# Rows of cumulated decays: spread by matmuls, or fetched from DRAM over GpSimd's queue

## The chip, the cores and the metric

The kernel runs on one core of a Trainium2 chip. The metric is the device time of one execution in microseconds; of several runs the median is given.

## The reference

One residual layer of a streaming encoder on 1024 positions of width 1024, with 16 meta tokens ahead of them (1040 columns in all). Two token mixers work on the same normalised input: a Mamba-2 SSD (32 heads of 64 channels, 4 groups, state 128) and a gated DeltaNet (16 value heads, 8 query and key heads, 128 channels each). Their gated outputs are merged, projected and followed by a SwiGLU feed-forward block and a last RMSNorm. What matters here is one term of both mixers. Each head has a log decay per position, which is cumulated along a chunk, and inside a chunk every pair of positions l and s is weighted with the exponential of the difference:

```
diff = a_cum[..., :, None] - a_cum[..., None, :]
segsum_exp = jnp.exp(jnp.where(mask, diff, -jnp.inf))
scores = cb[:, :, :, None] * segsum_exp(a_cum)      # SSD
a_low = where(strict, (k_beta k^T) * decay, 0)      # DeltaNet, with decay = segsum_exp(g_cum)
qk = (q k^T) * decay
```

The kernel takes chunks of 128 positions: chunks 0 to 7, and chunk 8, which holds the 16 meta tokens and comes first.

## The kernel before, in words

**Stages.** The input is normalised and kept as two tiles, u_hi and u_lo, so that a product in float32 is made of three passes (`dense`, lines 143 to 145: high by high, low by high, high by low). First comes the tile with the decays and betas ("dab"), whose columns are turned into tokens by head (lines 308 to 356): the result is `cum` [128, 9, 48], the cumulated log decays of the 32 SSD heads and the 16 DeltaNet heads for nine chunks. Then DeltaNet runs in 8 sub-blocks of two value heads (`dn_conv`, `dn_p1`, `dn_inv`, `dn_meta`, `dn_merge`, `dn_p2`, `dn_z`), then SSD in 4 groups of 8 heads (`ssd_conv`, `ssd_chunk`, `ssd_z`, `ssd_norm`), then the branch projections, the output projection and the feed-forward block.

**Where the decay is made.** `decay` (line 420) needs, in every partition s, the row of cum over the positions l. The preparation (lines 359 to 374) transposes cum into rows, splits each row into three bf16 parts and stacks the parts in `rowS` and `rowD` [96, 1040]. In `decay` one matmul per head (line 424) multiplies a column of ones at that head's three rows, `selS` or `selD`, broadcast over 128 columns, with the chunk's part of the rows: every partition of a PSUM bank then holds the row. ScalarE computes the positive part of cum[s] - row[l] from PSUM into the tile E (line 427, Relu with scale -1 and bias cum) and then exp(-E) in place (line 430). In DeltaNet (`dn_p1`) the bank is shared with k k^T and k q^T, there are two heads per chunk, and E (eight buffers) lives until `dn_p2` of the same chunk has used it. In SSD (`ssd_chunk`) a chunk has two tiles Es of four heads each (three buffers), each from a bank of the tag "p"; ScalarE also makes `ec`, the exponential of the rows themselves, from the same bank (line 764), VectorE multiplies Es with the masked C B^T (line 765), and TensorE reads Es at line 777.

**What sets the order.** The program text gives priorities. The framework that builds the kernel places the instructions of each engine by these priorities, by data and buffers, and by its own forecast of durations; the order per engine is then fixed, each engine runs its queue in order, and semaphores are put in for dependences. So TensorE's queue is a mixture of a small step of DeltaNet or SSD and of dense products of other tiles that fill the gaps. Weight tiles come on SP's queue (`load_w`, line 135), with one tile ahead. GpSimd does little: in this part the memsets of raw (line 383), ss (445), X (556) and T32 (576).

**Chain of a DeltaNet sub-block.** `dn_p1` makes the blocks W of nine chunks, W goes to DRAM in 32 x 32 blocks (line 547), comes back as X (557), is inverted by 30 steps on VectorE (563, 565), goes out and back once more (567, 573), is merged on TensorE (593 to 612), and `dn_p2` runs through the chunks in order.

## Time and profile before

| | |
|---|---|
| median of 3 runs | 2938.79 us (2936.38 to 2939.13) |
| the profiled execution's own time | 2935.63 us |
| its span, first to last instruction | 2933.8 us |
| mean granted TensorE clock | 0.99 of full speed |
| TensorE / VectorE / ScalarE / GpSimd busy | 97% / 66% / 41% / 180 us |
| DMA | 227 MB, mean 77 GB/s |

In the views PE is TensorE's matmuls, PEld its weight loads (beside the matmuls), DVE VectorE, ACT ScalarE, POOL GpSimd, SP SyncE and SPq its queue of DMA issues. L424 is line 424 of the kernel. `out<-in` are tiles by the program's names, with partitions x elements and the type. A busy share is an average over stages, so stretches are read by themselves: start and end of a stretch in us from the span's start.

### The profile page before, as it was taken

The page shows a single profiled execution, that of the slowest core. Times are in us where ns is not written, and L with a number is a line of the kernel's source. Part 1 is how long each engine was busy: PE and PEld are TensorE (multiplying, and loading weights), DVE is VectorE, ACT ScalarE, POOL GpSimd, SP SyncE. Part 2 cuts the span into 40 slices and gives each one's busy share as a digit, 9 for nine tenths or more (in the row PEclk, how much of TensorE's full clock was granted, in tenths as well). Part 3 has the DMA queues.
Part 4 walks back from the last instruction along what each step waited for, and adds up shares of the span by engine and source line. Part 5 has one row for each costly group of instructions (what it writes and reads, how often), then busy time and mean ns, then how long its engine had stood idle before and what let it go on. Part 6 is the DMA issues. An engine that isn't in the chain of part 4 may idle for free.

```text
span 2933.8 us, 41854 instructions
## 1 busy us (share of the span) xinstructions
PE 2848.0 (97%) x15921; PEld 2420.8 (83%) x15921; DVE 1938.7 (66%) x3788; ACT 1203.0 (41%) x2856; POOL 180.4 (6%) x190
## 2 busy tenths in 40 slices
PE   8999999999999799999999999999999899999998
PEld 7888888898888689878888778888877788887887
DVE  7768687696876755867777653564668655556446
ACT  5645445354354344645555543222235233333212
POOL 2000000000000000000000000000100432230000
PEclk9999999999999999999999999999999999999999
DMA  3111121111211111121111124342453222226312
GB/s 101 51 58 44 44 66 37 51 52 30 73 44 44 60 50 44 37 71 38 51 45 47 69 80 158 108 160 91 138 167 105 98 81 86 86 79 223 97 50 83
DMA packets 120273, 227.27 MB, mean 77 GB/s; under 512 B 48088, under 2 KB 54904, under 8 KB 120072
## 3 DMA queue, kind: packets, MB, share of 16 engines
q1 hardware_dynamic: 119496, 224.07, 23.2%
q8 instruction: 125, 2.05, 0.3%
q14 instruction: 76, 0.62, 0.1%
q10 hardware_dynamic: 576, 0.52, 0.1%
HBM read 175.16 MB, written 49.38 MB: 77 GB/s over the span
## 4 chain that ended last, share of the span: by engine, by line
PE 83%; ACT 7%; DVE 6%; DMA 3%; issue 1%; SPq 0%; POOL 0%; DVEq 0%; POOLq 0%; ACTq 0%
PE psd L143 15%; PE psd L144 15%; PE psd L145 15%; PE pq_p L1038 1%; PE pq_p L1039 1%; PE pq_p L1040 1%; ACT Es L427 1%; PE ps_p L593 1%; PE pq_psd L1040 1%; PE pq_psd L1039 1%; PE pq_psd L1038 1%; PE ps_a L639 1%; PE ps_a L651 1%; PE ps_o L661 1%; PE ps_o L777 1%
## 5 line engine op out<-in xcount | busy, mean ns | idle before, releaser
L143 PE MATMUL psd<-u_hi,whi 128*128 128x512 f32 (+3 forms) x2136 | 759.8, 356 | 10.7 <-ACT raw L382 10.2
L144 PE MATMUL psd<-u_lo,whi 128*128 128x512 f32 (+3 forms) x2136 | 755.1, 354 | 3.7 <-DVE u_lo L152 2.7
L145 PE MATMUL psd<-u_hi,wlo 128*128 128x512 f32 (+3 forms) x2136 | 753.2, 353 | 1.7 <-DVE wlo L137 1.7
L143 PEld LDWEIGHTS psd<-u_hi,whi 128*128 128x128 f32 x2136 | 402.7, 189 | 51.7 <-ACT raw L382 15.9
L136 ACT CAST whi<-wraw 128x1024 fp32r<-128x1024 f32 (+2 forms) x197 | 187.9, 954 | 610.7 <-PE psd L144 430.0
L144 PEld LDWEIGHTS psd<-u_lo,whi 128*128 128x128 f32 x2136 | 402.8, 189 | 40.4 <-DVE u_lo L152 4.1
L145 PEld LDWEIGHTS psd<-u_hi,wlo 128*128 128x128 f32 x2136 | 403.2, 189 | 36.5 <-DVE wlo L137 2.4
L137 DVE TENSOR_TENSOR wlo<-wraw,whi 128x1024 fp32r<-128x1024 f32 (+2 forms) x197 | 219.0, 1112 | 121.0 <-ACT whi L136 118.6
L145 PE MATMUL psd<-blk,wlo 128*128 128x512 f32 x512 | 199.3, 389 | 0.0
L143 PE MATMUL psd<-blk,whi 128*128 128x512 f32 x512 | 199.2, 389 | 0.0
L144 PE MATMUL psd<-blk,whi 128*128 128x512 f32 x512 | 199.2, 389 | 0.0
L382 ACT COPY raw<-psd 128x256 f32<-128x256 f32 x165 | 73.2, 444 | 113.8 <-PE psd L145 111.8
L942 DVE TENSOR_TENSOR part<-part,psd 128x512 f32<-128x512 f32 x96 | 65.6, 683 | 74.3 <-PE psd L145 74.3
L145 PEld LDWEIGHTS psd<-blk,wlo 128*128 128x128 f32 x512 | 96.1, 188 | 20.2 <-DVE wlo L137 0.3
L144 PEld LDWEIGHTS psd<-blk,whi 128*128 128x128 f32 x512 | 96.1, 188 | 20.1
L143 PEld LDWEIGHTS psd<-blk,whi 128*128 128x128 f32 x512 | 96.1, 188 | 19.8
L1022 POOL TENSOR_TENSOR sw<-wraw 128x512 f32<-128x512 f32 x42 | 63.3, 1507 | 377.3 <-DMA wraw<-w_gu 377.3
L563 DVE TENSOR_TENSOR itmp<-X 66x30 f32<-66x30 f32 (+14 forms) x240 | 78.1, 326 | 6.5 <-DMA X<-nd 1.0
L565 DVE TENSOR_TENSOR X<-X,itmp 66x30 f32<-66x30 f32 (+14 forms) x240 | 78.1, 325 | 6.0
L427 ACT ACTIVATE Es<-ps_p,cum 128x128 f32<-128x128 f32 x256 | 73.5, 369 | 2.5 <-PE ps_p L424 1.7
L399 ACT ACTIVATE zt<-psd 128x512 f32<-128x512 f32 x64 | 38.1, 596 | 88.4 <-PE psd L145 66.1
L725 DVE TENSOR_TENSOR cbm<-ps_p,tri 128x128 f32<-128x128 f32 x32 | 9.3, 291 | 87.2 <-PE ps_p L723 87.0
(682 smaller groups left out, 5857.2 us busy)
## 6 DMA issues: line engine op xcount, KB each, us to landing
wraw<-w_in SPq DMA_DIRECT2D x105, 512.0 KB
wraw<-w_gu SPq DMA_DIRECT2D x48, 512.0 KB
wraw<-w_br SPq DMA_DIRECT2D x36, 512.0 KB
c<-hc SPq DMA_DIRECT2D x22, 512.0 KB
hc<-c SPq DMA_DIRECT2D x22, 512.0 KB
wraw<-w_dn SPq DMA_DIRECT2D x40, 256.0 KB
g<-zt SPq DMA_DIRECT2D x32, 256.0 KB
y_d<-zt SPq DMA_DIRECT2D x32, 256.0 KB
```

Source lines behind the costliest of these rows:

```text
L136: act.copy(hi[:, 0:kk], raw[:, 0:kk])
L137: dve.tensor_tensor(lo[:, 0:kk], raw[:, 0:kk], hi[:, 0:kk], op=ALU.subtract)
L143: pe.matmul(ps[:, 0:n], hi[:, wk0 + k], ahi(k), start=(k == 0), stop=False)
L144: pe.matmul(ps[:, 0:n], hi[:, wk0 + k], alo(k), start=False, stop=False)
L145: pe.matmul(ps[:, 0:n], lo[:, wk0 + k], ahi(k), start=False, stop=(k == kk - 1))
L382: dense_u((name, lambda ps, p0, p1: act.copy(raw[:, 3 + p0:3 + p1], ps)))
L427: act.activation(E[0:L, i, 0:L], ps[0:L, 128 * i:128 * i + L], AF.Relu, bias=cum[0:L, c, h0 + h:h0 + h + 1], scale=-1.0)
L563: dve.tensor_tensor(t, X[:, 0:j, j:j + 1].broadcast_to([66, j, m]), X[:, j:j + 1, j + 1:32].broadcast_to([66, j, m]), op=ALU.mult)
L565: dve.tensor_tensor(X[:, 0:j, j + 1:32], X[:, 0:j, j + 1:32], t, op=ALU.add)
L942: dve.tensor_tensor(part[:, m, cs], part[:, m, cs], ps, op=ALU.add)
L1022: eng.tensor_tensor(t, x, y, op=op)
L1038: pe.matmul(ps, w[0][:, k], y[0][:, k], start=start and k == 0, stop=False, skip_group_check=not start)
```

## The change

The preparation now makes only nine transposes of cum (48 heads at once), copies them into one tile of float32 rows, and stores it to a DRAM tensor of 48 rows. `spread` fetches the rows of n heads for one chunk with a DMA on GpSimd's queue straight into the tile E, broadcast over the partitions; `decay` then works in place on E. In DeltaNet `dn_rows` allocates E and issues the fetch; `dn_p1s` issues the first three chunks ahead of the first `dn_p1` and then the chunk two ahead. In SSD `ssd_rows` does the same for the next chunk ahead of the present one, with four buffers of Es in place of three, and `ec` is taken from the fetched rows before `decay` overwrites them. rowS, rowD, the selectors and their input are gone.

```
@@ body
+    cum_dram = dram.tile([48, TT], F32, name="cum_d")
...
-        for row, h0 in ((rowD, 16), (rowS, 0)):
-            c3 = sb.tile([128, 9, 3, 32], F32, name="c3")
-            pool.tensor_copy(c3, cum[:, :, h0:h0 + 32].unsqueeze(2).broadcast_to([128, 9, 3, 32]))
-            rr = sb.tile([96, TT], F32, name="rr")
-            b2 = sb.tile([96, TT], BF16, name="b2")
-            for c in range(9):
-                c0, L = (NM + 128 * c, 128) if c < 8 else (0, NM)
-                ps = psm("p")
-                pe.transpose(ps[0:96, 0:L], V(c3[0:L, c], "p a b -> p (a b)"), ident[0:L, 0:L])
-                act.copy(rr[:, c0:c0 + L], ps[0:96, 0:L])
-            for i in range(3):
-                r32 = slice(32 * i, 32 * i + 32)
-                act.copy(row[r32], rr[r32])
-                if i < 2:
-                    dve.tensor_copy(b2, rr)
-                    dve.tensor_tensor(rr, rr, b2, op=ALU.subtract)
+        rr = sb.tile([48, TT], F32, name="rr")
+        for c in range(9):
+            c0, L = (NM + 128 * c, 128) if c < 8 else (0, NM)
+            ps = psm("p")
+            pe.transpose(ps[0:48, 0:L], cum[0:L, c], ident[0:L, 0:L])
+            act.copy(rr[:, c0:c0 + L], ps[0:48, 0:L])
+        sp.dma_start(cum_dram, rr)
...
-    def decay(E, ps, row, sel, h0, hs, c):
+    def spread(E, h0, n, c):
         c0, L = cr(c)
-        for i, h in enumerate(hs):
-            pe.matmul(ps[0:L, 128 * i:128 * i + L], sel[:, h:h + 1].broadcast_to([96, L]),
-                      row[:, c0:c0 + L], start=True, stop=True)
-        for i, h in enumerate(hs):
-            act.activation(E[0:L, i, 0:L], ps[0:L, 128 * i:128 * i + L], AF.Relu,
-                           bias=cum[0:L, c, h0 + h:h0 + h + 1], scale=-1.0)
-        n = len(hs)
+        pool.dma_start(E[0:L, 0:n, 0:L], cum_dram[h0:h0 + n, c0:c0 + L].unsqueeze(0).broadcast_to([L, n, L]))
+
+    def decay(E, h0, n, c):
+        c0, L = cr(c)
+        for i in range(n):
+            act.activation(E[0:L, i, 0:L], E[0:L, i, 0:L], AF.Relu, bias=cum[0:L, c, h0 + i:h0 + i + 1], scale=-1.0)
         act.activation(E[0:L, 0:n, 0:L], E[0:L, 0:n, 0:L], AF.Exp, scale=-1.0)
...
+    def dn_rows(i, c):
+        E = sub[i]["E", c] = (sb.tile([128, 2, 128], F32, name="E", bufs=8) if c < 8 else
+                              sb.tile([NM, 2, NM], F32, name="Em"))
+        spread(E, 32 + 2 * i, 2, c)
@@ dn_p1
-            E = d["E", c] = sb.tile([128, 2, 128], F32, name="E", bufs=8)
-        else:
-            E = sb.tile([NM, 2, NM], F32, name="Em")
-        decay(E, ps, rowD, selD, 32, (2 * i, 2 * i + 1), c)
+        E = d["E", c]
+        decay(E, 32 + 2 * i, 2, c)
...
+    def ssd_rows(g, c):
+        if c == 8 or g == NGRP or (g, c) in ssd_E:
+            return
+        E = ssd_E[g, c] = [sb2.tile([128, 4, 128], F32, name="Es", bufs=4) for _ in range(2)]
+        for q in range(2):
+            spread(E[q], 8 * g + 4 * q, 4, c)
@@ ssd_chunk
+        ssd_rows(g, c)
+        ssd_rows(*((g, (c + 1) % 9) if c != 7 else (g + 1, 0)))
...
-        E = [sb2.tile([128, 4, 128], F32, name="Es", bufs=3) for _ in range(2)]
+        E = ssd_E.pop((g, c))
         for q in range(2):
-            pd = psm("p")
-            decay(E[q], pd, rowS, selS, 0, range(8 * g + 4 * q, 8 * g + 4 * q + 4), c)
-            pd = V(pd, "p (a b l) -> p a b l", a=2, b=2)
+            pd = V(E[q], "p (a b) l -> p a b l", b=2)
             for b in range(2):
                 r = slice(64 * b, 64 * b + 64)
                 act.activation(ec[r, 2 * q:2 * q + 2], pd[r, :, b], AF.Exp)
+            decay(E[q], 8 * g + 4 * q, 4, c)
@@ dn_p1s
-        for c in (8, *range(8)):
+        cs = [8, *range(8)]
+        for n, c in enumerate(cs):
+            for c2 in cs[n + 2:n + 3] if n else cs[0:3]:
+                dn_rows(i, c2)
             dn_p1(i, c)
```

## Rows read from the trace of the kernel before

**Rows 1.** The page, its first section: busy us (share of the span) xinstructions.
```profile
PE 2848.0 (97%) x15921; PEld 2420.8 (83%) x15921; DVE 1938.7 (66%) x3788; ACT 1203.0 (41%) x2856; POOL 180.4 (6%) x190
```

**Rows 2.** Busy time by stretch: length, each engine's busy us, clock, DMA share, GB/s.
```profile
100.00:950.00 850.00, 829.92 (x5512) 732.35 (x5510) 631.81 (x1687) 400.53 (x1238) 20.76 (x51) 1.00 0.17 49
950.00:1000.00 50.00, 33.84 (x187) 26.21 (x186) 38.94 (x149) 21.45 (x87) 0.00 (x0) 0.86 0.13 38
...
1160.00:1725.00 565.00, 559.67 (x3529) 474.09 (x3528) 409.76 (x697) 305.74 (x711) 1.60 (x16) 1.00 0.15 51
```

**Rows 3.** Line 424 by itself: count, ns min/median/max, first and last start.
```profile
L424 PEld LDWEIGHTS <-selS x256: 95/97/102, 1172.7 to 1720.6; 96*128 96x128 bf16 x128
...
L424 PEld LDWEIGHTS <-selD x144: 87/100/152, 92.7 to 980.3; 96*128 96x128 bf16 x128, 96*16 96x16 bf16 x16
```

**Rows 4.** Timeline of TensorE in SSD: start us, duration us, line, tiles, count.
```profile
1334.01 0.28 PE L143 MATMUL psd<-u_hi,whi 128*128 128x256 f32 x1
1334.13 0.40 PE L424 MATMUL ps_p<-rowS,selS 96*128 96x128 bf16 x4
...
1334.54 0.28 PE L145 MATMUL psd<-u_hi,wlo 128*128 128x256 f32 x1
...
1348.33 0.39 PE L424 MATMUL ps_p<-rowS,selS 96*128 96x128 bf16 x4
1348.56 0.61 PE L734 MATMUL ps_z<-ident,xt 128*128 128x128 f32 x4
1349.00 1.06 PE L770 MATMUL ps_b<-Ct,Ss 128*128 128x128 f32 x8
...
1350.25 0.28 PE L143 MATMUL psd<-u_hi,whi 128*128 128x256 f32 x1
1350.58 0.38 PE L424 MATMUL ps_p<-rowS,selS 96*128 96x128 bf16 x4
1350.77 0.36 PE L144 MATMUL psd<-u_lo,whi 128*128 128x256 f32 x1
1350.97 0.28 PE L145 MATMUL psd<-u_hi,wlo 128*128 128x256 f32 x1
```

**Rows 5.** Timeline of TensorE in DeltaNet, one pair and what follows it.
```profile
346.85 0.28 PE L424 MATMUL ps_p<-rowD,selD 96*128 96x128 bf16 x2
346.96 0.44 PE L524 MATMUL ps_p<-qk 128*128 128x128 f32 x2
```

**Rows 6.** Groups of ScalarE by line and shape: count, busy us, mean ns, idle before.
```profile
L764 ACT ACTIVATE ec<-ps_p 64x256 f32<-64x256 f32 x128 | 48.3, 377 | 1.6
...
L430 ACT ACTIVATE E<-E 128x256 f32<-128x256 f32 x64 | 27.1, 423 | 0.6
```

**Rows 7.** TensorE's waits in the SSD stretch: us in total, times, longest.
```profile
PE ps_a L746 <- ACT xh L148: 4.3, 14, 0.4
```

**Rows 8.** A store's issue and its waiter, from the timeline; VectorE's waits for W.
```profile
183.20 0.33 SPq L567 DMA_DIRECT2D xd<-X  x1
...
186.34 1.39 POOL L576 MEMSET T<- 128x1536 f32 x1 [26.28 <-DMA xd<-X]
...
DVE T L580 <- DMA W<-xd: 27.5, 18, 6.3
```

**Rows 9.** Timeline of DeltaNet's sub-block 1, its last chunk: E released, E's Relu.
```profile
243.68 0.38 PE L661 MATMUL ps_o<-v,E 128*128 128x128 f32 x2
...
248.60 0.62 ACT L427 ACTIVATE E<-ps_b,cum 128x128 f32<-128x128 f32 x2
```

**Rows 10.** Timeline of the preparation, and ScalarE's group of row copies.
```profile
79.44 1.88 POOL L361 COPY c<-cum 128x864 f32<-128x864 f32 x1 [4.75 <-DVE cum L352]
...
123.12 0.17 DVE L477 TENSOR_TENSOR w<-dtb,ss 128x18 f32<-128x18 f32 x1
...
L368 ACT COPY rr<-ps_p 96x128 f32<-96x128 f32 x16 | 3.5, 261 | 1.2 <-PE ps_p L367 1.2
```

**Rows 11.** GpSimd's groups: the memset of raw, count, busy, idle before it.
```profile
L383 POOL MEMSET raw<- 128x3 f32 x56 | 5.6, 100 | 938.6 <-DVE qk L388 305.6 <-DVE Ct L388 271.9 <-DVE xt L388 207.8
```

More of the change, by code (lines that the diff above doesn't have):

```diff
@@ L225, in body @@
     dte = tkp.tile([128, 9, 48], F32, name="dte")
-    rowS = tkp.tile([96, TT], BF16, name="rowS")
-    rowD = tkp.tile([96, TT], BF16, name="rowD")
-    selS = tkp.tile([96, 32], BF16, name="selS")
-    selD = tkp.tile([96, 16], BF16, name="selD")
     convp = tkp.tile([128, len(CONV), 5], F32, name="convp")
@@ L297, in body @@
         dve.tensor_scalar(dnw, dnw, 0.5, None, op0=ALU.mult)
-        s0 = sb.tile([96, 48], F32, name="s0")
-        sp.dma_start(s0, A["c_sel"])
-        dve.tensor_copy(selS, s0[:, 0:32])
-        dve.tensor_copy(selD, s0[:, 32:48])
         alog = sb.tile([128, 48], F32, name="alog")
@@ L708, in ssd_conv @@
         conv_tile(name, d["x"][:, j % 4])
+    ssd_E = {}
+    def ssd_rows(g, c):
[4 more added lines that the diff above has]
+            spread(E[q], 8 * g + 4 * q, 4, c)
     def ssd_chunk(g, c):
+        ssd_rows(g, c)
+        ssd_rows(*((g, (c + 1) % 9) if c != 7 else (g + 1, 0)))
         d = grp[g]
@@ L1272, in prepare @@
     d["c_stri"] = np.triu(np.ones((128, 128), np.float32), 1)
-    sel = z(96, 48)
-    for i in range(3):
-        sel[32 * i:32 * i + 32, 0:32] = np.eye(32)
-        sel[32 * i + 16:32 * i + 32, 32:48] = np.eye(16)
-    d["c_sel"] = sel
     return d
```

## The prediction

> **What bounds the kernel now.** I read the page first, for the engines' shares: TensorE is busy for 97% of the span [rows 1]. That is an average over stages, so the next view is the busy time by stage. In the stretch of DeltaNet from 100 to 950 us TensorE works 829.9 of 850 us; where DeltaNet's last sub-block begins, 950 to 1000 us, it works only 33.8 of 50; in the SSD stretch, 1160 to 1725 us, it works 559.7 of 565 [rows 2]. ScalarE is at 306 and VectorE at 410 of those 565 us, and DMA has a share of 0.15. So in SSD nothing that leaves TensorE's queue is covered by other work: it comes off the end, as long as nobody begins to keep TensorE waiting. In DeltaNet the same holds except in the 50 us stretch, where a chain of small steps sets the pace.
>
> The third view is the changed line itself. L424 spreads one row of cumulated decays over 128 partitions, once per head and chunk: 256 matmuls for SSD and 144 for DeltaNet, 400 in all [rows 3].
>
> **What is removed.** In SSD the 256 matmuls stand in 64 groups of four. Ahead of SSD's own transposes a group takes 0.23 us, from 1348.33 to the next instruction at 1348.56 [rows 4]. In the middle of dense products it takes more than its own slots: dense products of this form follow each other every 0.12 us, and around one group two of them plus the group take 0.53 us (1334.01 to 1334.54), around another 0.72 us (1350.25 to 1350.97) [rows 4], so the group displaces 0.29 or 0.48 us. I count 31 groups of the dense kind and 33 of the other. With the middle of the two examples, 0.385 us, this is 31 x 0.385 + 33 x 0.23 = 11.9 + 7.6 = 19.5 us. The lower end, if only the bare slots come free (0.19 us at 1350.58, [rows 4]), is 64 x 0.19 = 12 us; the upper end is 31 x 0.48 + 7.6 = 22.5 us.
>
> In DeltaNet a pair takes 0.11 us (346.85 to 346.96) [rows 5], and there are 72 pairs: 7.9 us. One sub-block in eight lies where TensorE has idle time anyway, so I take 7/8 of it, 6.9 us; the ends are 0 (if DeltaNet's chain sets the pace everywhere) and 7.9.
>
> In the preparation 18 transposes become 9. A transpose of a 128-column tile takes a quarter of the 0.44 us between 1348.56 and 1349.00 [rows 4], so about 1.0 us goes. The split into three bf16 parts on ScalarE and VectorE, the two copies on GpSimd (1.88 us, [rows 10]) and the load of the selectors also go. They ran beside TensorE's dense products, so I cost them at nothing; were that cover gone, they would add some us to the gain, not to the loss. The sum removed is 19.5 + 6.9 + 1.0 = 27.4 us.
>
> **What is added.** *ScalarE reads SBUF where it read PSUM.* Exponentials of 256 columns take 377 ns from PSUM and 423 ns from SBUF [rows 6], 46 ns more. With 400 Relu and 128 exponentials that is 24 us of ScalarE, 17.7 of it in SSD. ScalarE has room, and TensorE waited for it only 4.3 us in all of SSD [rows 7]. But inside a chunk ScalarE runs through its fourteen instructions of the decay without a pause, and the products with Es wait at its end. I take 4 us of the 24; the ends are 0 and 24.
>
> *The rows travel by DMA on GpSimd's queue.* No GpSimd DMA is in this trace. The nearest row for a transfer is the 264 KB store of X: issued at 183.20 (0.33 us), GpSimd goes on at 186.34, 3.1 us later [rows 8]. The longest single wait for a transfer to land is 6.3 us, for W's blocks [rows 8]. For the issue itself the lower end is SP's 0.33 us, the upper GpSimd's longest step in the rows here, the 1.88 us copy [rows 10]. I take 0.33 and 3.1, 3.4 us together, since a block of rows (128 KB in DeltaNet, 256 KB in SSD) is nearest in size to that store; the range keeps 8.2 us. The Trainium skill ("DMA: Bandwidth & Descriptors", section "Anatomy of one DMA — SWDGE (gpsimd) path") gives 2.0 us plus the bytes at 436 GB/s; by it DeltaNet's fetch would take an estimated 2.3 us, and the sum would stay as it is.
>
> *Where it is hidden.* In SSD 36 chunks share the 565 us [rows 2], 15.7 us each, and the fetch for the next chunk can start when the chunk before this one has freed its two tiles (four buffers now): at either end, two fetches of 1.9 us issue each are covered. In DeltaNet "two chunks ahead" is the order of issue; tiles E have eight buffers, so chunk c of the next sub-block can only be fetched once dn_p2 has read chunk c of this one. For the last chunk of sub-block 1 that is 243.68 plus 0.38 = 244.06 us, and ScalarE takes up that chunk's Relu at 248.60 [rows 9]. The lead is 4.5 us: 1.1 us to spare at 3.4 us, 3.7 us late at 8.2 us. Seven sub-blocks have such a tail: 0 to 26 us. I take 3 us, because TensorE still has dense tiles to put there. If that cover is gone, as at 950 to 1000 us, what is late next is W, its store and the inversion.
>
> *The first fetch.* GpSimd's copy shows cum ready at 79.44; nine copies of 0.26 us [rows 10], a store and a fetch of 3.4 us each are done some 12 us later even if they don't overlap. The first reader on VectorE needs w, written at 123.12 [rows 10]. Even behind one more weight load on SP the slack of over 25 us holds: nothing. The weight loads that queue behind the store on SP wait for at most the end of the nine copies, in a stretch where each weight tile is loaded one tile ahead; I cost this at nothing too.
>
> *DMA.* SSD fetches 64 blocks of 256 KB, 16.8 MB in 565 us or 30 GB/s beside 51 GB/s at a share of 0.15 [rows 2]: about 0.09 more. That delays no weight load.
>
> **Sum.** 27.4 - 4 - 3 = 20.4 us. The profiled execution took 2935.6 us (its span is 2933.8), which leaves 2915.2; the median of the runs is 3.2 us above it, hence 2918.
>
> **Rivals.** *A, the gain is given back:* DeltaNet's chain sets the pace. For: the period of a sub-block is one chain through dn_p1, the inversion and dn_p2, and at 950 us it is bare. Against: 98% busy over 850 us. Then DeltaNet's 6.9 us is lost, the tails cost 8 us and ScalarE 8: 20.5 - 16 = 4.5 us faster, 2934.
>
> *B, slower: fetches held in GpSimd's queue.* That queue is strictly in order, and it also carries the memsets of raw (56, which wait 938.6 us in all, 16.8 each [rows 11]) and of T and X; one of them sat 26.28 us until a DMA had landed [rows 8]. A fetch behind such a memset is late, ScalarE stops at the Relu of L427 with the PSUM copies of L382 behind it, and TensorE runs out of banks. Price: one held fetch for each of seven sub-blocks, 16.8 less the lead of 4.5, is 12.3 x 7 = 86 us against 20: 3004; with half that delay 2961. It decides from 20.4 / 7 = 2.9 us per sub-block on. Against it: today these memsets wait for buffers long before anybody needs them, and the order on the queue follows when work is expected to be ready. The Trainium skill ("SBUF — State Buffer", section "SBUF: two separate sides") has a second cause for late fetches: GpSimd writes its DMA descriptors through a port that VectorE locks in its two-port modes. No run here shows it yet; by that rule the delay would end up in the same tails.
>
> *C, the order does not follow:* the build places instructions by its own forecast of their times, so what leaves TensorE may come back as waits elsewhere, or the new order may fill some of the 16 us that are idle at 950 to 1000 us. This widens both ends by a few us. That rows are simply not prefetched is part of A.
>
> **How the numbers follow.** Forecast (2903 to 2930) 0.62; better than that 0.04; A (2930 to 2940) 0.17; B (2945 and up, half of it under 2965) 0.17. The low end of the range is the upper ends without costs: 22.5 + 7.9 + 1.0 = 31.4 off, 2907, and 5 us for the order: 2902. The high end, 2950, takes in A and the mild part of B, and leaves out about 2 in 10. A measurement of this kernel can tell 0.2%, 5.9 us, from no change: under 2933 is faster, over 2945 slower. That gives 0.71 faster, 0.12 same, 0.17 slower.
>
> **What would show it.** Right: L424's matmuls gone, TensorE's busy time down by some 25 us, its share still about 97%, waits of ScalarE for the rows near zero, and the SSD stretch shorter by 15 to 20 us. Wrong: a wait of ScalarE's L427 successor for a DMA of cum rows, longest in DeltaNet's later chunks; GpSimd busy for more than 2 us per fetch; a gap of TensorE at the end of each dn_p1; TensorE waiting for ScalarE in SSD for more than 10 us. A fetch that takes over 6 us to land makes the prediction fall.

## The result, and the profile after

The change made the kernel slower: 3016.04 us (median of 4 runs, 3010.72 to 3019.77) against 2938.96 us (4 runs) for the kernel before, a ratio of 1.0266 with a 95% interval of 1.0253 to 1.0278. The forecast was 2918 us, the range 2902 to 2950. The profiled execution has a span of 3009.0 us where the kernel before has 2933.8.

In the page, first section (engines: busy us, share, instructions), TensorE is the line to compare with [rows 1]:

```profile
PE 2842.1 (94%) x15512; PEld 2422.6 (81%) x15512; DVE 1945.4 (65%) x3778; ACT 1226.5 (41%) x2841; POOL 273.3 (9%) x324
```

TensorE's busy time fell by 5.9 us only, and its idle time rose from 85.8 to 166.9 us. By stretch (length, busy us of PE, PEld, DVE, ACT, POOL, clock, DMA share, GB/s), against [rows 2]:

```profile
100.00:950.00 850.00, 793.94 (x5194) 692.62 (x5192) 627.40 (x1693) 395.19 (x1207) 60.64 (x106) 0.98 0.21 56
950.00:1000.00 50.00, 46.19 (x263) 40.15 (x263) 40.04 (x114) 23.05 (x74) 2.70 (x5) 0.97 0.23 53
1160.00:1800.00 640.00, 580.21 (x3419) 508.41 (x3419) 425.87 (x709) 325.40 (x694) 46.58 (x78) 0.95 0.38 71
```

In SSD TensorE now stands for 60 of 640 us, and the mean granted clock is 0.95 where it was 1.00. Of the two levels, 1.2 and 2.4 GHz, it is mostly the upper one; the lower one comes where TensorE has just stood (same view, TensorE alone: length, busy us, clock, DMA share, GB/s):

```profile
1560.00:1564.00 4.00, 0.60 (x4) 0.85 0.92 72
1564.00:1568.00 4.00, 3.12 (x9) 0.50 0.11 12
1568.00:1572.00 4.00, 4.00 (x20) 0.79 0.00 0
1572.00:1576.00 4.00, 4.00 (x29) 1.00 0.41 131
```

The three groups of dense products take longer by it: the same 2136 instructions each, 759.8, 755.1 and 753.2 us before, now

```profile
L143 PE MATMUL psd<-u_hi,whi 128*128 128x512 f32 (+3 forms) x2136 | 771.9, 362 | 19.6 <-DVE zt L384 15.7
L144 PE MATMUL psd<-u_lo,whi 128*128 128x512 f32 (+3 forms) x2136 | 763.3, 357 | 3.8 <-DVE u_lo L152 2.8
L145 PE MATMUL psd<-u_hi,wlo 128*128 128x512 f32 (+3 forms) x2136 | 763.2, 358 | 3.7 <-DVE wlo L137 3.7
```

which is 30.3 us more. The selector matmuls did leave the queue. That TensorE's busy time hardly fell has two reasons: the records of matmuls that follow each other overlap, so that without the selector matmuls' own records it would have been 2840.3 us before, 7.7 less; and the dense products now take longer (by less than 30.3 us of the span, since they overlap too).

Stage by stage, by the issue of the last y_d store, the last y_s store, and the end: 1091.8, 1768.3, 2933.8 us before; 1100.5, 1841.9, 3009.0 after. From mark to mark DeltaNet takes 8.7 us longer, SSD 64.9 (676.5 to 741.4), the rest 1.6. The marks don't cut TensorE's work at the same place, though. In the trace of the kernel before, 53 dense products more lie ahead of the last y_d store than in the change, where they follow it. At the 0.12 to 0.18 us from one such product to the next in that trace they are an estimated 9 us, so at equal work DeltaNet loses about 18 us and SSD about 56. Most of the loss is SSD's, where the forecast had its largest gain.

The waits say where (engine, what it makes, line, waited for: us in total, times, longest):

```profile
ACT ec L760 <- DMA Es<-cum_d: 120.0, 37, 6.2
...
ACT E L413 <- DMA E<-cum_d: 50.7, 45, 2.7
...
POOL Es L407 <- PE ps_o L774: 360.4, 20, 40.8
...
POOL E L407 <- PE ps_o L648: 228.7, 44, 14.9
...
PE ps_o L774 <- DVE xdt L735: 37.5, 18, 3.2
PE ps_o L648 <- ACT v L644: 19.4, 23, 2.4
```

ScalarE waits 170.7 us for fetched rows, and GpSimd waits for TensorE to release the tiles before it can issue a fetch. The waits for released tiles cost nothing by themselves. TensorE's two waits at the end are what reaches the critical engine; the first is new, and the second stood at 3.8 us (5 times) before.

One chunk of SSD, from the timelines of TensorE, GpSimd and ScalarE (start, duration, engine, line):

```profile
1409.45 1.09 PE L774 MATMUL ps_o<-Es,xdt 128*64 128x128 f32 x16
...
1410.41 1.49 POOL L407 DMA_DIRECT2D Es<-cum_d  x2 [10.88 <-PE ps_o L774]
...
1411.66 0.60 ACT L148 CAST xh<-xde 128x512 fp32r<-128x512 f32 x1
1416.21 0.86 ACT L760 ACTIVATE ec<-Es 64x256 f32<-64x256 f32 x2 [3.95 <-DMA Es<-cum_d]
1417.10 1.29 ACT L413 ACTIVATE Es<-Es,cum 128x128 f32<-128x128 f32 x4
```

The product with Es, py (L774), frees two Es tiles, GpSimd fetches at once, and ScalarE, which has the decay of those rows next in its fixed order, stops until they land. VectorE does not read the result before 1437.53, some 21 us later. Nobody needs the rows when ScalarE waits for them; what is needed is the work behind. VectorE's and TensorE's timelines, one chunk on:

```profile
1440.82 1.30 DVE L370 SCALAR_TENSOR_TENSOR xt<-raw,convp,xt 128x1040 f32<-128x1040 f32 x1 [2.00 <-ACT xt L368]
...
1443.45 0.69 DVE L735 TENSOR_TENSOR xdt<-ps_z,dtb 128x512 f32<-128x512 f32 x1
...
1444.19 0.98 PE L774 MATMUL ps_o<-Es,xdt 128*64 128x128 f32 x14 [1.99 <-DVE xdt L735]
```

ScalarE's convolution step (L368) is late, so VectorE's step on it is late (29.2 us of such waits between 1160 and 1800 us, 14 times), xdt behind it is late, and TensorE stops at py with dense products behind.

### The profile page after: what moved, and what is told of

It is laid out like the page before. It is cut to its first block, busy times and chain, and to the rows that moved or that the text cites. A ratio compares the mean times of both kernels' runs of the same rounds, so it can differ in the third digit from the quotient of the medians.

```text
span 3009.0 us, 41265 instructions
## 1 busy us (share of the span) xinstructions
PE 2842.1 (94%) x15512; PEld 2422.6 (81%) x15512; DVE 1945.4 (65%) x3778; ACT 1226.5 (41%) x2841; POOL 273.3 (9%) x324
## 4 chain that ended last, share of the span: by engine, by line
PE 63%; DVE 12%; issue 9%; DMA 8%; ACT 6%; POOL 1%; SPq 1%; POOLq 0%; DVEq 0%; ACTq 0%
PE psd L145 11%; PE psd L143 11%; PE psd L144 11%; DMA Es<-cum_d 5%; DMA E<-cum_d 2%; ACT Es L413 1%; PE pq_p L1038 1%; PE pq_p L1039 1%; PE pq_p L1040 1%; PE pq_psd L1038 1%; PE pq_psd L1039 1%; PE pq_psd L1040 1%; PE ps_p L580 1%; PE pq_psd L143 1%; PE pq_p L143 1%
## 5 line engine op out<-in xcount | busy, mean ns | idle before, releaser
L143 PE MATMUL psd<-u_hi,whi 128*128 128x512 f32 (+3 forms) x2136 | 771.9, 362 | 19.6 <-DVE zt L384 15.7
L144 PE MATMUL psd<-u_lo,whi 128*128 128x512 f32 (+3 forms) x2136 | 763.3, 357 | 3.8 <-DVE u_lo L152 2.8
L145 PE MATMUL psd<-u_hi,wlo 128*128 128x512 f32 (+3 forms) x2136 | 763.2, 358 | 3.7 <-DVE wlo L137 3.7
L143 PEld LDWEIGHTS psd<-u_hi,whi 128*128 128x128 f32 x2136 | 410.5, 192 | 57.2 <-DVE zt L384 18.0
L145 PEld LDWEIGHTS psd<-u_hi,wlo 128*128 128x128 f32 x2136 | 410.4, 192 | 40.7 <-issue 4.9
L144 PEld LDWEIGHTS psd<-u_lo,whi 128*128 128x128 f32 x2136 | 409.8, 192 | 38.7 <-DVE u_lo L152 4.2
L145 PEld LDWEIGHTS psd<-blk,wlo 128*128 128x128 f32 x512 | 96.1, 188 | 22.4 <-DVE wlo L137 2.4
L144 PEld LDWEIGHTS psd<-blk,whi 128*128 128x128 f32 x512 | 96.1, 188 | 19.9
L143 PEld LDWEIGHTS psd<-blk,whi 128*128 128x128 f32 x512 | 96.1, 188 | 19.8
L760 ACT ACTIVATE ec<-Es 64x256 f32<-64x256 f32 x128 | 53.2, 416 | 126.7 <-DMA Es<-cum_d 120.0
L407 POOL DMA_DIRECT2D Es<-cum_d x64 | 47.7, 750 | 565.6 <-PE ps_o L774 360.4
L651 DVE SCALAR_TENSOR_TENSOR S<-S,clast,ps_a 128x128 f32<-128x128 f32 x128 | 39.1, 344 | 70.5 <-PE ps_a L646 70.3
L413 ACT ACTIVATE Es<-Es,cum 128x128 f32<-128x128 f32 x256 | 83.4, 393 | 1.6
```

The costliest lines, as they stand in the source:

```text
L143: pe.matmul(ps[:, 0:n], hi[:, wk0 + k], ahi(k), start=(k == 0), stop=False)
L144: pe.matmul(ps[:, 0:n], hi[:, wk0 + k], alo(k), start=False, stop=False)
L145: pe.matmul(ps[:, 0:n], lo[:, wk0 + k], ahi(k), start=False, stop=(k == kk - 1))
L413: act.activation(E[0:L, i, 0:L], E[0:L, i, 0:L], AF.Relu, bias=cum[0:L, c, h0 + i:h0 + i + 1], scale=-1.0)
```

## The experiments

The table gives all runs in their order: median, ratio to the kernel before with its interval, and the stage marks of the profiled execution (last y_d store, last y_s store, span). Each ratio is against runs of the kernel before made beside it, whose medians lie between 2934.99 and 2938.96 us.

| Run | us | ratio | y_d | y_s | span |
|---|---|---|---|---|---|
| before | 2938.96 | | 1091.8 | 1768.3 | 2933.8 |
| the change | 3016.04 | 1.0266 [1.0253, 1.0278] | 1100.5 | 1841.9 | 3009.0 |
| contig | 2941.72 | 1.0025 [1.0015, 1.0036] | 1115.8 | 1774.4 | 2939.5 |
| pitch | 2968.74 | 1.0117 [1.01, 1.0134] | 1128.0 | 1797.5 | 2966.5 |
| bufs6 | 2924.16 | 0.9964 [0.9954, 0.9974] | 1101.0 | 1755.9 | 2920.4 |
| ssd_only | 2998.79 | 1.0217 [1.0202, 1.0233] | 1095.0 | 1831.7 | 2997.1 |
| ssd6 | 2908.74 | 0.9908 [0.9893, 0.9924] | 1103.7 | 1748.1 | 2913.4 |
| one6 | 2926.9 | 0.9968 [0.9956, 0.9981] | 1102.0 | 1757.8 | 2923.8 |
| dn_e12 | 2924.63 | 0.995 [0.9937, 0.9964] | 1102.4 | 1758.0 | 2923.6 |
| all12 | 2925.9 | 0.9964 [0.995, 0.9978] | 1113.6 | 1753.3 | 2919.2 |
| dn_only | 2989.42 | 1.0184 [1.0168, 1.0199] | 1147.6 | 1824.4 | 2991.9 |
| dn_ring | 2927.18 | 0.9962 [0.9948, 0.9976] | 1104.2 | 1760.2 | 2927.5 |
| all_ssd | 2904.95 | 0.9897 [0.9882, 0.9911] | 1095.7 | 1735.5 | 2901.6 |
| dn_behind | 2885.11 | 0.9823 [0.9808, 0.9838] | 1065.1 | 1714.2 | 2878.6 |
| all_behind | 2903.85 | 0.9894 [0.9876, 0.9912] | 1091.9 | 1732.8 | 2897.4 |
| ssd4_behind | 2942.52 | 1.0025 [1.0015, 1.0035] | 1100.4 | 1771.1 | 2938.1 |
| before_behind | 2934.73 | 0.9999 [0.9989, 1.0008] | 1093.3 | 1769.9 | 2935.5 |
| both4 | 2905.39 | 0.9892 [0.9877, 0.9907] | 1068.9 | 1737.1 | 2903.6 |
| both6 | 2907.36 | 0.9898 [0.9881, 0.9914] | 1069.3 | 1739.0 | 2906.3 |

**The order of the queues.** An edit binds one thing, and the build then lays out the queue of every engine by its own forecast. What it made of each edit can be read from the traces, as the order in which an engine's instructions start:

- *SSD.* contig, pitch and ssd_only have the change's order on TensorE and VectorE, and on ScalarE but for 9 of its 764 instructions. The runs with six Es tiles keep TensorE's and VectorE's order too, but more of ScalarE's instructions stand elsewhere (80 of 767 in bufs6). ssd4_behind, both4 and both6 share an order of their own, with instructions of TensorE and VectorE elsewhere as well (468 of 3943 and 273 of 758, ssd4_behind against the change).
- *DeltaNet.* The change, bufs6, one6, dn_e12, dn_ring and ssd4_behind have one order. contig, pitch and dn_only have a second (all but some 40 of TensorE's 6595 instructions alike). dn_behind, both4 and both6 have a third, in which 1247 of TensorE's 6541 instructions and 411 of VectorE's 2077 stand elsewhere than in bufs6. ssd_only, ssd6 and all_ssd have a fourth; all12 and all_behind have one each.

So a difference between runs of one order is due to the fetch or the buffers; between runs of different orders it may also come from where the other engines' work stands. bufs6, one6, dn_e12 and dn_ring, which have the same orders, lie within some 3 us of each other: smaller differences say nothing.

**The transfer.** Two runs change only how the rows lie in DRAM.

contig, a chunk's rows side by side, one piece per partition and fetch (cut: the store and `spread` follow the layout):

```diff
-    cum_dram = dram.tile([48, TT], F32, name="cum_d")
+    cum_dram = dram.tile([9, 48, 128], F32, name="cum_d")
...
```

> The DRAM tensor is laid out by chunk (9, 48, 128), so that the rows of a fetch lie side by side: one piece of 2 KB per partition in SSD and of 1 KB in DeltaNet, where it was four and two pieces of 512 bytes. Theory 1 (small pieces fill the DMA engines, so rows land later than the build forecast, and ScalarE, in order, stands at them): the landing of Es falls from 6.2 us to 3.5 or less, ScalarE's wait for Es from 120 us to under 40, and the time to 2910 to 2945. Rival 2 (fetches are held in GpSimd's queue or start too late for want of buffers): the time stays above 2985.

pitch, pieces of 512 bytes as in the change, each now on a multiple of 512 bytes (cut in the same way):

```diff
-    cum_dram = dram.tile([48, TT], F32, name="cum_d")
+    cum_dram = dram.tile([48, 9 * 128], F32, name="cum_d")
...
```

> The pieces stay 512 bytes, but the rows' pitch becomes 4608 bytes and every piece begins at a multiple of 512 bytes (before, 64 bytes beside one). If it is the number of pieces that makes a fetch slow, the landing stays at 5.5 to 6.5 us and the time at 3000 to 3020. If it is where they begin, the landing falls to 4 us or less, and the time by 40 us or more.

Landing times (KB each, median us) and the queue's share of 16 DMA engines, of the change, then pitch, then contig:

```profile
q0 software_dynamic: 8448, 25.19, 7.2%
...
Es<-cum_d POOLq DMA_DIRECT2D x64, 256.0 KB, 6.2
...
E<-cum_d POOLq DMA_DIRECT2D x64, 128.0 KB, 3.4
```

```profile
q0 software_dynamic: 8448, 25.19, 3.5%
...
Es<-cum_d POOLq DMA_DIRECT2D x64, 256.0 KB, 3.9
```

```profile
q0 software_dynamic: 8448, 25.19, 3.5%
...
Es<-cum_d POOLq DMA_DIRECT2D x64, 256.0 KB, 3.6
```

With the pieces aligned the 256 KB land 2.3 us earlier, with one piece per partition 2.6 us. ScalarE's wait in SSD falls from 120.0 us to 66.1 (pitch, 27 times) and to

```profile
ACT ec L765 <- DMA Es<-cum_d: 60.0, 28, 3.8
```

in contig, where I had expected under 40. SSD shrinks to 669.5 us (pitch) and 658.6 us (contig). The order of the queues in SSD is the change's, so the slow landing alone accounts for contig's 82.8 us (about 74 at equal work, since contig has the 53 dense products ahead of the mark). At the same TensorE work as before, contig's SSD is 17.9 us under the kernel before. DeltaNet, however, is longer than in the change (1128.0 and 1115.8), so that even contig is no gain. The build gave it another order there, so this says nothing on what the landing does in DeltaNet. The slow landing is one condition of SSD's loss; the next runs show that it is not the only one.

**Buffers and lead in SSD.** bufs6 has six Es tiles and asks for rows two chunks ahead:

```diff
-        E = ssd_E[g, c] = [sb2.tile([128, 4, 128], F32, name="Es", bufs=4) for _ in range(2)]
+        E = ssd_E[g, c] = [sb2.tile([128, 4, 128], F32, name="Es", bufs=6) for _ in range(2)]
...
-        ssd_rows(*((g, (c + 1) % 9) if c != 7 else (g + 1, 0)))
+        for a, b in [x for x in seq[seq.index((g, c)) + 1:] if x[1] != 8][0:2]:
+            ssd_rows(a, b)
```

> Layout as in the changed kernel, but six buffers of Es in place of four, and rows fetched two chunks ahead in SSD. Rival 2 (the fetch starts too late, since its buffers are held by the products of two chunks ago): ScalarE's wait for Es falls under 40 us and the time under 2960. Theory 1: the build again places the decay as soon as it forecasts the rows, so the landing stays at about 6 us, ScalarE waits for Es over 80 us, and the time stays above 2985.

The landing stayed long (6.8 us), ScalarE's wait for Es fell from 120.0 us to

```profile
ACT ec L762 <- DMA Es<-cum_d: 5.8, 3, 3.8
```

and SSD took 654.9 us, 21.6 less than before the change. The rows now have time: from the issue of a chunk's first fetch to its first reader on ScalarE it is 16.7 us in the median, where the change has 5.9, the landing itself. one6 has the six tiles (the first of the two edits) but the change's place in the program:

> Six buffers of Es, but the program still asks for rows one chunk ahead. If buffers set when a fetch can start, it behaves like two chunks ahead: ScalarE's wait for Es under 20 us and 2918 to 2932. If the place in the program sets it, the wait stays over 80 us and the time over 2980.

It gave the same within 3 us, and the build made the same queues of it: the buffers did it, not the line where the fetch stands.

**The stages apart.** ssd_only and ssd6 keep DeltaNet's matmuls (`decay` with rowD and selD as before the change) and fetch for SSD alone, with four and six buffers; dn_only does the reverse. Of ssd_only's edit (against the change, cut), DeltaNet's part:

```diff
...
-        E = d["E", c]
-        decay(E, 32 + 2 * i, 2, c)
+            E = d["E", c] = sb.tile([128, 2, 128], F32, name="E", bufs=8)
+        else:
+            E = sb.tile([NM, 2, NM], F32, name="Em")
+        decay(E, ps, rowD, selD, 32, (2 * i, 2 * i + 1), c)
...
```

> SSD fetches its rows as in the changed kernel, DeltaNet spreads them by matmuls as before. By the stages of the two profiles SSD carries +65 us and DeltaNet +9, so 3000 to 3012 is expected. If DeltaNet's fetches cost more than its stage shows, the time is under 2985; if the two stages only shift waits, it is over 3015.

> DeltaNet spreads its rows by matmuls as before; SSD fetches them, with six buffers of Es and two chunks ahead. Theory 2 (in SSD the matmuls' removal is a gain once the fetch has buffers; in DeltaNet the fetch costs more than it saves): SSD takes 650 to 660 us where it took 677 before, DeltaNet ends at 1088 to 1096 us, and the time is 2908 to 2920, below that of the run with six buffers and fetches in both (2924). If DeltaNet's fetches are no loss, the time is 2924 or more.

> DeltaNet's rows are fetched as in the change, SSD keeps its matmuls. Theory (DeltaNet's fetch loses by itself): the last y_d store came 9 us later than before with the change and 3 us later with SSD alone changed, and against the version with matmuls in DeltaNet and six SSD buffers the fetch costs 12 to 18 us (2924.2, 2926.9 against 2908.7); some 2945 to 2953 us, ScalarE waiting about 50 us for E over some 45 fetches. Rival (the forecast's own sum for DeltaNet, the loss lying in what SSD did to the gates placed between): about 2929 to 2933 us.

In ssd_only SSD takes 736.7 us, so its loss needs nothing of DeltaNet (the time, 2998.79 us, is just under the range that I gave). With six buffers the same fetch wins, 0.9908; its profiled execution is the slowest of its four, and the stages in it (1103.7 us, then 644.4) are not in the ranges that I gave. The result of dn_only was worse than any theory said: SSD takes 676.8 us, as before the change, and DeltaNet 55.8 us more than before. TensorE stands for 21.8 us between 1000 and 1060 us there, in the last sub-block's bare stretch.

contig, pitch and dn_only have nearly one order in DeltaNet and fetch with landings of 3.2, 3.4 and 3.5 us, and there the wait can be seen at work. TensorE's wait for v in the three:

```profile
PE ps_o L653 <- ACT v L649: 20.2, 23, 2.7
PE ps_o L649 <- ACT v L645: 25.8, 28, 2.0
PE ps_o L684 <- ACT v L680: 32.6, 30, 2.7
```

DeltaNet is 24.0, 36.2 and 55.8 us longer than before. Between contig and pitch, which differ in nothing but how the rows lie in DRAM, 0.2 us per fetch grow to 12.2 us of DeltaNet, more than these waits hold. What else makes dn_only the longest stays open.

all_ssd adds the side-by-side rows, the edit of contig, to ssd6:

> Matmuls in DeltaNet as before, SSD's fetch with six buffers two chunks ahead, rows laid side by side in DRAM, so that a fetch lands in about 3.6 us and not 7.2. Theory (with the buffers there, the landing is hidden): 2905 to 2912 us, the same as without the layout. Rival (the long transfers also cost by keeping the DMA engines busy for the weight loads): under 2903 us, with less wait of TensorE and ScalarE for weights.

3.7 us instead of 7.2 to land moved the time by 4 us, within the spread of the runs (ssd6 alone goes from 2905 to 2915 us): with the buffers there, the landing is hidden.

**More E tiles.** dn_e12 is bufs6 with twelve E tiles (`bufs=12`), all12 has the side-by-side rows too, and dn_ring makes the tiles go round twelve fixed places. dn_ring's edit beside that of bufs6 (cut):

```diff
-        E = sub[i]["E", c] = (sb.tile([128, 2, 128], F32, name="E", bufs=8) if c < 8 else
+        E = sub[i]["E", c] = (sb.tile([128, 2, 128], F32, name="E", tag=f"E{(8 * i + c) % 12}", bufs=1) if c < 8 else
...
```

> As the run with six buffers of Es (2924), and DeltaNet's E gets twelve buffers in place of eight, so that the rows of the next sub-block's first four chunks don't wait for dn_p2 of this one. If DeltaNet's loss is the same want of buffers, ScalarE's wait for E falls from 51 us to under 30 and the time to 2905 to 2918. If only the last chunks' fetches are late (they still wait for dn_p2), the wait stays over 40 and the time at 2918 to 2930.

> Twelve buffers of E, six of Es with two chunks ahead, and the rows side by side in DRAM. If the parts add up, the landing of Es is 3.6 us and the time is 2895 to 2915. If landing no longer matters once there are buffers, the time equals that of the run with twelve and six buffers within 6 us.

> Six SSD buffers, two chunks ahead, and DeltaNet's tiles made to go round twelve fixed places; in the version with twelve buffers the fetches came at the same times as with eight (427.4 and 428.9 us, each waiting for line 648 in the chunk of the same number), so it did not test the lead. Theory (DeltaNet loses because each fetch starts only when phase 2 frees the tile, about a chunk before ScalarE wants it): GpSimd's wait for line 648 falls from 210 us to a few, ScalarE's wait for E from 50 us to under 10, and the time to 2906 to 2914 us. Rival (the order of ScalarE's work, not the wait itself, is what costs): the waits go and the time stays at 2921 to 2927 us.

None of them helped, and the waits hardly moved (44 and 41 fetches still wait for L648 in the change and in dn_ring, ScalarE 50.7 and 50.8 us; in all12, whose order is another, it is 37.9). Only the first fetches come earlier: once the tiles are full, each fetch again follows a release, and ScalarE takes up each decay as soon as the rows land, however far ahead that is. Longer rings therefore did not test the lead, and my expectation for them was wrong. What they pointed at was ScalarE's order.

**ScalarE's order.** In DeltaNet of the change one chunk goes like this (timelines of GpSimd, ScalarE, TensorE):

```profile
435.30 0.72 POOL L407 DMA_DIRECT2D E<-cum_d  x1 [5.59 <-PE ps_o L648]
...
438.88 0.70 ACT L413 ACTIVATE E<-E,cum 128x128 f32<-128x128 f32 x2 [0.57 <-DMA E<-cum_d]
439.60 0.63 ACT L644 ACTIVATE v<-ps_a,w 128x128 f32<-128x128 f32 x2
...
440.09 0.49 PE L648 MATMUL ps_o<-v,E 128*128 128x128 f32 x2
...
441.53 0.72 POOL L407 DMA_DIRECT2D E<-cum_d  x1 [4.52 <-PE ps_o L648]
```

That is a closed loop. TensorE's product with E (L648) releases a tile, the fetch follows, ScalarE waits for it, then makes v (L644), and only then can TensorE run the next L648. dn_behind is bufs6 with the decay put behind the last v of phase 2 one chunk further on. The edit binds ScalarE's order alone (no wait, no buffer, no arithmetic changed), but the build rearranged the other engines' queues in DeltaNet after it (cut):

```diff
+        with tc.issue_after(last_v[i - 1, min(c + 1, 7)].ins) if i and c < 8 else ExitStack():
-        decay(E, 32 + 2 * i, 2, c)
+            decay(E, 32 + 2 * i, 2, c)
...
```

> The version with six SSD buffers, two chunks ahead, and in DeltaNet the two Relus and the exponential of a chunk put behind the last v of phase 2 one chunk further on, on ScalarE's order alone; fetches, buffers and arithmetic as they are. Theory (DeltaNet's loss is ScalarE's place for the decay, right behind the forecast landing and ahead of line 644, which phase 2 on TensorE waits for): ScalarE's wait for E falls from 51 us (45) to under 15, TensorE's wait for line 644 from 19.5 us (23) to about the 4 us of the kernel before, and the time to 2900 to 2912 us. Rival (something else in DeltaNet costs, such as the fetches themselves or the fill that is taken from the last sub-block): the waits go and the time stays at 2919 to 2928 us.

all_behind is the same with contig's edit.

> The same order of DeltaNet's decays with six SSD buffers, eight DeltaNet buffers and the rows side by side in DRAM (landing 3.2 and 3.6 us instead of 3.4 and 6.8). Theory as in the run beside it, the landing being hidden in both: 2897 to 2910 us, within 5 us of it and at or below the 2905 us of the version with matmuls in DeltaNet. Rival: over 2915 us, so that DeltaNet is better left with its matmuls.

Of ScalarE's waits in dn_behind:

```profile
ACT E L413 <- DMA E<-cum_d: 14.1, 10, 2.5
```

ScalarE's wait went from 51.3 to 14.1 us, TensorE's wait for v (19.5 us, 23 times in bufs6) is gone, and the time fell by 39 us to 2885.11, more than expected and the best of all runs: 1.8% faster than the kernel before. The waits that went are less than the 39 us, and TensorE's and VectorE's queues are others, so how much of it is ScalarE's place and how much the new order isn't shown. all_behind, with the side-by-side rows, has as little waiting (12.8 us) but 2903.85 us, which I did not expect; its DeltaNet ends 26.8 us later. It has the same edit and again another order (1915 of TensorE's 6576 instructions stand elsewhere): short waits alone don't make DeltaNet fast.

ssd4_behind leaves the four buffers and the 512-byte pieces of the change and moves ScalarE's work in SSD behind the Bh cast of the same chunk (cut):

```diff
-        act.copy(Bh[0:L], ps[0:L, 0:128])
+        bh_i = act.copy(Bh[0:L], ps[0:L, 0:128])
...
+            with tc.issue_after(bh_i.ins):
...
```

> The change as it is, four SSD buffers, 512-byte pieces, with one thing moved: ScalarE's ec and decay of an SSD chunk stand behind the Bh cast of the same chunk in ScalarE's order, some 8 us later than in the change and still ahead of VectorE's product. Theory (the four buffers hurt only through the place that ScalarE's work takes right behind the forecast landing): ScalarE's wait for Es falls from 120 us to under 30, and the time to 2920 to 2940 us. Rival (with four buffers the fetch itself comes too late, whatever ScalarE's order): the wait stays and the time with it, over 2980 us.

The waits of ScalarE and GpSimd there:

```profile
ACT E L413 <- DMA E<-cum_d: 49.5, 42, 2.4
...
POOL Es L407 <- PE ps_o L775: 410.0, 51, 35.8
```

Of ScalarE's waits for rows only E's is left; the 120.0 us for Es are gone. The fetches still follow a release (51 waits for L775) and land in 5.4 us, but from the first fetch's issue to its first reader it is now 26.5 us. SSD shrinks from 741.4 to 670.7 us; the time, 2942.52 us, is just above the range that I gave. VectorE's and TensorE's queues in SSD are others here too, so the 70.7 us are not the reader's place alone.

Three more runs use the same two edits: before_behind, meant as a control (the kernel before, with DeltaNet's move around its own `decay`), both4 (the change with both moves and its own buffers), and both6 (both moves and bufs6's edit).

> A control: the kernel before, matmuls and all, with the same move of DeltaNet's decays on ScalarE's order (behind the last v of phase 2 one chunk further on). Theory (the move only takes away a wait that the fetch brought): no wait for a fetch is here to be removed, so 2930 to 2942 us. Rival (the move improves DeltaNet's order by itself, the fetch having little part in the 39 us that it gave): 2895 to 2915 us.

> The change with its own four SSD buffers, eight DeltaNet buffers and 512-byte pieces; only ScalarE's order is moved, in both stages (DeltaNet's decay behind v one chunk further on, SSD's ec and decay behind the Bh cast of the chunk). Theory (ScalarE's place for the decays is the whole loss): the 73 us that the move gave in SSD and the 39 us that it gave in DeltaNet add up, 3016 - 73 - 39, so 2898 to 2910 us, faster than the kernel before. Rival (the two overlap or the four buffers keep something back): over 2920 us.

> Both moves of ScalarE's order with six SSD buffers, two chunks ahead. Theory (with six buffers ScalarE's wait in SSD is gone already, so the move there has nothing left to take away): within 6 us of the 2885 us of the version with the move in DeltaNet alone. Rival (SSD's order still costs with six buffers): under 2878 us.

The control is 0.9999 [0.9989, 1.0008], but it controls nothing: in its trace every engine's instructions stand in the order of the kernel before. The kernel before has DeltaNet's decays behind that v already. So it was the change that brought them ahead of it, and dn_behind puts them back; whether the move would help without a fetch stays untested. both4, which asks for nothing but the two moves on ScalarE, came in at 2905.39 us, some 110 us below the change and 1.1% faster than the kernel before. both6 missed both its theories, 22 us above dn_behind. Its SSD takes 669.7 us against 649.1, and one wait on VectorE is there that dn_behind does not have (SSD stretch of both6):

```profile
DVE Es L768 <- ACT Es L414: 13.5, 24, 0.9
```

Behind the Bh cast the decay ends just as VectorE wants it, so with six buffers this place is too late rather than too early. The same wait and nearly the same SSD (670.7 and 668.2 us) are in ssd4_behind and both4: the three have one order, and in it the number of buffers makes no difference. How much of the 20 us over dn_behind is this wait and how much TensorE's and VectorE's other order wasn't followed further.

## Why the prediction was wrong

**The step that failed** is "Where it is hidden", in both stages. In SSD it said that the fetch "can start when the chunk before this one has freed its two tiles (four buffers now): at either end, two fetches of 1.9 us issue each are covered". The start is right, it is what GpSimd's waits on L774 show. The cover is wrong: it set the fetch against the 15.7 us of a whole chunk. It has to be set against the place of the first reader in its engine's fixed order, and ScalarE's decay stands a few us behind the issue. The cost of this was put at nothing in SSD and was 64.9 us (about 56 at equal work). At the forecast's own landing it would have done little harm in SSD (contig, 3.6 us: 17.9 us shorter, against the 15 to 20 that I expected). The forecast gain would not have come even so: with the landing about as forecast contig takes 2941.72 us and not 2918, for its DeltaNet is 24.0 us longer than before. Each of three edits takes SSD's loss away: a fast landing (contig, 82.8 us back) and an earlier issue with a third pair of tiles (bufs6, 86.5), both with TensorE's and VectorE's order kept, and the reader's place together with the order that the build made of it (ssd4_behind, 70.7). The text did say that the build orders by its own forecast, but only as rival C, worth a few us; here it decided the sign.

In DeltaNet the step looked only at the last chunk of each sub-block and took 3 us, "because TensorE still has dense tiles to put there". It also took the lead from the place of the Relu in the kernel before, 4.5 us behind the release, where the change has the decay at 3.5 us behind the issue, just where the rows land. In the trace 44 fetches wait for L648, so nearly every chunk has such a tail, and ScalarE's 50.7 us stand in front of v. dn_behind against bufs6 puts the price of that order at 39 us in all; the part of it that is the wait is not separated.

**The size of the landing.** I took 3.4 us for both fetches; E's is 3.4, Es's 6.2 (the range kept 8.2). The prediction said that a fetch of over 6 us makes it fall. With the four tiles and the order of the change it did. It need not: bufs6 lands in 6.8 us and is faster than the kernel before, ssd6 in 7.2 us and is 0.9% faster. The issue on GpSimd took 0.72 us for E and 0.75 for Es, between my two ends. The Trainium skill ("DMA: Bandwidth & Descriptors", section "Anatomy of one DMA — SWDGE (gpsimd) path") gives an estimated 2.6 us for 256 KB and 2.3 us for 128 KB, by 2.0 us plus the bytes at 436 GB/s; the trace has 6.2 and 3.4, and the measurement decides. The DMA share was undersized too: 0.09 more was forecast, and from 1160 to 1800 us it went from 0.19 to 0.38.

**What was removed** was, if anything, more than the 27.4 us of the sum. In dn_behind, where TensorE is no longer stopped and the clock is 0.991, its busy time is 45.8 us below the kernel before's. The selector groups of the kernel before were, by their own busy time,

```profile
L424 PE MATMUL ps_p<-rowS,selS 96*128 96x128 bf16 x256 | 24.8, 219 | 0.7
...
L424 PE MATMUL ps_p<-rowD,selD 96*128 96x128 bf16 x64 | 9.2, 219 | 0.0
...
L424 PE MATMUL ps_b<-rowD,selD 96*128 96x128 bf16 x64 | 9.0, 222 | 0.0
```

43.0 us together, but as their records overlap those of their neighbours, that the two numbers lie close shows nothing. My way, by how much a group pushes its neighbours apart, gave 19.5 us in SSD. The runs with six buffers whose SSD holds the same dense products as before are 32.1 (ssd6) to 36.8 us (all12) shorter there, with the buffers and the order of the queues in that number too. In DeltaNet it gave 6.9 us, and dn_behind gained 26.7. Of that, about 12 us is the bare stretch of the last sub-block: from 900 to 1000 us TensorE is busy for 83.8 us before and 96.1 in dn_behind. The rest wasn't taken apart.

**What ScalarE adds** looks right and is so by luck: 24 us were forecast, and its busy time went from 1203.0 to 1226.5. ec takes 416 ns instead of 377 [rows 6], Es's Relu 393 instead of 369, E's 396 instead of 368: 14.7 us in all, not 24. The 46 ns came from two instructions on different numbers of partitions (64 and 128). With the copies that left the preparation, the durations of all of ScalarE's instructions add up to 4.6 us more; its busy time rose by more because its records overlap less. That the products with Es would suffer for it did not show.

**The first fetch** and the preparation cost nothing that can be seen, as forecast: in the first 100 us TensorE works for 89.4 us, and for 89.9 before.

**The rivals.** B had the sign and, for SSD, the middle of its mechanism: ScalarE stopped in its order with other work behind. Its cause was wrong. In SSD GpSimd's queue held no chunk's fetch behind a memset: those that follow one had waited 6.9 us or more of their own since. In DeltaNet three of 64 came within 0.4 us of a memset that had itself waited (4.3 to 6.3 us). B's 2961 to 3004 us stopped short of 3016. The second cause that I named for it, VectorE locking GpSimd's port (the Trainium skill, "SBUF — State Buffer", section "SBUF: two separate sides"), left no mark on the issues: with VectorE busy for 65% of the span, the 64 issues for Es took

```profile
L407 POOL DMA_DIRECT2D Es<-cum_d x64: 749/749/767, 1098.3 to 1775.5; - x64
```

(ns min/median/max). Rival A, DeltaNet giving its gain back, did happen, as 8.7 us of 75.2 by the marks (about 18 at equal work). So did a part of C: the new order filled the bare stretch, 46.2 us of TensorE's work between 950 and 1000 us where the kernel before has 33.8 [rows 2]. It was far too little.

## What to carry to other kernels

A transfer is hidden only if it lands before its *first reader's place in that engine's order*, not before the result is wanted; where the build orders by forecast times, look up what stands behind that reader and who needs it. Replacing a producer that could never be late by a DMA turns a buffer's release into a possible stop of the in-order engine, so give it buffers for the whole way from issue to last use, or put the reader later. Binding the reader's place touches no data and was worth 110 us here. But where a build lays out all queues by a forecast, look up in the trace what else it moved before an edit's result is put down to the edit, and whether a control differs from its original at all.

## What was not expected of the hardware

The start of the 512-byte pieces mattered for the four-row fetches and not for the two-row ones. Rows 4160 bytes apart, so that most pieces start off a multiple of 256 bytes, took 6.3 us for 256 KB and 5.7% of the DMA engines' time for SSD's 16.78 MB (ssd_only); side by side it was 3.7 us and 1.9% (all_ssd). While such a fetch ran, the DMA engines were full and moved little (the change; the last two columns are DMA share and GB/s):

```profile
1412.00:1413.00 1.00, 1.00 (x7) 0.90 (x6) 1.00 (x2) 0.26 (x1) 0.00 (x0) 1.00 1.05 106
1413.00:1414.00 1.00, 1.00 (x7) 0.98 (x6) 1.00 (x3) 0.00 (x0) 0.10 (x1) 1.00 0.93 86
```

For DeltaNet's 128 KB the landing is 3.4 us in either alignment. The Trainium skill ("DMA: Bandwidth & Descriptors", section "How a descriptor splits into AXI transactions") has extra beats for pieces that start off a multiple of 256 bytes; by it a 512-byte piece here takes an estimated 16 to 22 beats, by where it starts, instead of 16, at most 1.4 times as long. The share of the engines rose threefold in SSD, so the rule goes the right way and is far from the size; what makes the difference between two rows and four stays open. The four-row fetches also go out in pairs and the two-row ones singly, and no run separates that.

The other surprise was the clock as a multiplier of stops: with TensorE busy for 94% of the span instead of 97%, the mean granted clock went from 0.990 to 0.977, and the 30.3 us that the records of the same dense products grew by stand beside a loss of 75.2 us in the span.
